# Earlier evacuation of one retention key group, a feed-forward product kept in SBUF, and a reordered exit

## The chip, the cores and the metric

The kernel runs on one core of one Trainium2 chip. The metric is the time of one execution in microseconds, as the median of three runs. The engines are PE (TensorE, with weight loads shown apart as PEld), DVE (VectorE), ACT (ScalarE), POOL (GpSimd) and SP (SyncE, which issues most transfers).

## The reference

A trunk of two layers over 512 tokens of 1024 channels, in float32. Each layer projects the normalised input once, gives the columns to four token mixers of 256 channels each, projects their outputs back and adds them; then a SwiGLU feed-forward part of 2816 hidden channels.

```python
for l in range(DEPTH):                      # DEPTH = 2
    h = rms_norm(x, norm_mix_w[l])
    proj = h @ w_in[l]
    (rq, rk, rv, rg, ca, cg, gq, gk, gv, gg, gb, ga, hq, hf, hi, hgate) = split(proj)
    ret  = head_group_norm(retention_mixer(rq, rk, rv)) * silu(rg)
    conf = conformer_conv_mixer(ca, cg, ...)          # glu, 31 causal taps, layer norm, swish
    gdn  = head_rms_norm(gated_deltanet_mixer(...)) * silu(gg)
    hg   = head_rms_norm(hgrn2_mixer(hq, hf, hi, ...)) * silu(hgate)
    x = x + concat([ret, conf, gdn, hg]) @ w_out[l]
    h = rms_norm(x, norm_ffn_w[l])
    x = x + (silu(h @ ffn_w_gate[l]) * (h @ ffn_w_up[l])) @ ffn_w_down[l]
return rms_norm(x, final_norm_w)
```

## The kernel before

Activations lie with the channels on the 128 partitions and the 512 tokens along the free axis, so a group of 256 channels is two tiles (rk0 and rk1, rq0 and rq1, and so on). Each dense product is made of three matmuls on operands split into a high and a low part: high by high, high by low, low by high (lines 461 to 463; lines 486 to 488 in the form with tokens on the partitions, used for gg, hi, hgate, rv and rg). ScalarE makes the high part of a weight (lines 257 and 383), POOL or VectorE the low part (258 and 384).

**The order of a layer's front.** The projections run in a fixed list, gk, gq, gg, gv, hf, hq, hi, ca0, cg0, ca1, cg1, hgate, rk0, rk1, rq0, rq1, rv, rg. The four mixers gdn (delta rule), hgrn, conf (convolution) and ret (retention) are generators; inside a dense product, after each two contraction steps, `tick()` lets every running mixer write one more step. So the mixers' small products are written in between the dense ones. A mixer starts when its last input is there, ret behind rv. A scheduler that works from its own model of durations then settles the order of instructions on each engine.

**Buffers.** Eight PSUM banks: four of pool `pd` for dense results, four of pool `pm` for all else. conf keeps the glu that its taps read in a `pd` bank too. Tiles in SBUF come from an arena with a size limit; before a dense result is evacuated, the table `NEED` says how many tiles of 2 or 4 KB a partition must be free, by the first two letters of the group's name. If they aren't, `tick()` is called until they are, so mixers' steps come ahead of that evacuation. `rk=(2, 2, 2, 2)` asks for four tiles: cosine and sine by the norm's root, made once at rk0, and two tiles for the rotation. At rk1 the first two exist already.

**The steps that the prediction names.** Rotation of a retention group (`ev_rot`): four ScalarE copies of 32 partitions (727, 728), the product with the cosine on VectorE (729), two POOL operations (730, 731). conf's taps for one half of its channels: 23 operations on VectorE that read the glu (1292), seven on ScalarE (1296) with sums on POOL (1298), and the sum of both (1302). The delta rule's rounds that solve its triangular system: 1051, 1055 and 1062 on TensorE, with copies on VectorE (1057) and ScalarE (1053, 1065) between. Retention's state and outputs: 1387, 1417, 1422, 1429. Norm of a mixer's output: small factors on POOL (213, 771, 775), the product on POOL (781), the gate on VectorE (783), and the turn back to channels on partitions on TensorE (792); then the output projection starts.

**The feed-forward step.** `step` makes a pair of products of two block matrices with seven products in place of eight (Strassen's scheme as changed by Winograd): e, t1, t2, g, h, t3, t4. It runs 52 times, 26 in each layer. `ab` and `cd` are two `pm` banks, LO and UP their halves of 256 columns. t4 of a step is put off: `finish()` writes it behind the first two products of the next step. ScalarE copies t1 from `ab` to `cd` (1650), and the sum of e, t2 and t3 to a tile u3 (1659), which VectorE adds to the upper half of `cd` (1660).

**The exit.** `leave(half)` spreads the root of the norm over the partitions for 256 tokens (two matmuls at 242, a ScalarE copy at 246), multiplies eight tiles (five on VectorE from PSUM, three on POOL from SBUF) and sends each out with a transfer of 128 KB, on ScalarE's and SP's queues by turns.

Of the kernel before, what the change touches and what calls it, by code (L numbers as in the profile page):

```python
# [7 lines left out]
F32 = mybir.dt.float32  # L8
# [8 lines left out]
P = 128  # L17
T = 512
NB = T // P
D = 1024  # L20
KD = D // P
# [117 lines left out]
def kernel(  # L139
# [14 lines left out]
    nc = tc.nc  # L154
    V, S, GP, PE = nc.vector, nc.scalar, nc.gpsimd, nc.tensor
    MUL, ADD, SUB = ALU.mult, ALU.add, ALU.subtract
# [23 lines left out]
    x = [const.tile([P, T], F32, name=f"x{k}") for k in range(KD)]  # L180
# [4 lines left out]
    rsb = const.tile([P, T], F32, name="rsb")  # L185
# [40 lines left out]
    def rstd_sum(blocks, *tiles):  # L226

        ps = pm.tile([P, T], F32, name="pm")
        for n, t in enumerate(tiles):
            for b in blocks:  # L230
                PE.matmul(ps[:, b:b + 1], t[:, b * P:(b + 1) * P], ones[:, 0:1], start=(n == 0 and b == blocks[0]),
                          stop=(n == len(tiles) - 1 and b == blocks[-1]))
        r = slice(blocks[0], blocks[-1] + 1)
        ms = sm(NB, "ms")
        V.tensor_scalar(ms[:, r], ps[:, r], 1.0 / D, 1e-6, op0=MUL, op1=ADD)
        rsqrt_small(rst[:, r], ms[:, r], len(blocks))

    def rstd_spread(blocks=range(NB), half=True):

        pb = pm.tile([P, T], F32, name="pm")  # L240
        for b in blocks:
            PE.matmul(pb[:, b * P:(b + 1) * P], rst[:, b:b + 1].broadcast_to([P, P]), ident, start=True, stop=True)
        if half:
            V.tensor_scalar(rsh, rst, 0.5, None, op0=MUL)
        c = slice(blocks[0] * P, (blocks[-1] + 1) * P)
        S.copy(rsb[:, c], pb[:, c])
        return pb
# [194 lines left out]
    def start(l, name, gen):  # L442
        active.append([gen, (l, name), 0, lag_of((l, name), 0)])
# [5 lines left out]
    def tick():  # L449
        for it in list(active):  # L450
            if it[3] > 0:
                it[3] -= 1
            elif resume(it[0], it[1] + (it[2],)) == "end":
                active.remove(it)
            else:
                it[2] += 1
                it[3] = lag_of(it[1], it[2])
# [7 lines left out]
    def dense_c(ah, al, ks, ps=None):  # L465

        hv = w_next()
        if ps is None:
            ps = pd.tile([P, T], F32, name="pd")
        for n in range(KD):  # L470
            mm3(ps, *hv[n // 4], n % 4, ah[ks[n]], al[ks[n]], n == 0, n == KD - 1)
            if n % CHUNK_K == CHUNK_K - 1:
                tick()
        return ps
# [17 lines left out]
    def dense_c2():  # L492

        hv = [w_next(q) for q in range(2)]
        ps = [pm.tile([P, T], F32, name="pm") for _ in range(2)]
        for k in range(KD):
            for q in range(2):
                mm3(ps[q], *hv[q][k // 4], k % 4, xh[k], xl[k], k == 0, k == KD - 1)
            tick()
        return ps  # L500

    def dense_t(n):

        banks = [pd.tile([P, T], F32, name="pd") for _ in range(NB // 2)]
        ps = {b: (banks[b // 2][:, (b % 2) * n:(b % 2) * n + n], b % 2 == 0, b % 2 == 1) for b in range(NB)}
        for g in range(2):
            t_part(ps, w_next(), n, g, range(NB))
        return {b: ps[b][0] for b in range(NB)}

    def dense_t_wide(n):  # L510

        hv = []
        for part in range(2):
            blocks = range(2 * part, 2 * part + 2)
            ps = {b: (pd.tile([P, T], F32, name="pd")[:, :n], True, True) for b in blocks}
            for g in range(2):
                if part == 0:
                    hv.append(w_next(g))
                elif g:
                    w_ahead()  # L520
                t_part(ps, hv[g], n, g, blocks)
            yield {b: ps[b][0] for b in blocks}
# [9 lines left out]
    for k in range(KD):  # L532
        if k % 4 == 0:
            for p in range(2):
                c = slice(k * P, (k + 4) * P)
# [74 lines left out]
    def layer(l, ar, ga, open_mix, gvp, gzp):  # L610
# [56 lines left out]
        def ev_gg(ps4):  # L667
            if "bt" not in st:
                st["bt"], st["z"], st["gg"] = sm(NB * H, "bt"), sm(NB * H, "z"), ar.get(4)
            bt, z = st["bt"], st["z"]  # L670
            gate_t(ps4, st["gg"])
            for b in ps4:
                S.activation(bt[:, b * H:(b + 1) * H], ps4[b][:, G:G + H], AF.Tanh, scale=rsh[:, b:b + 1])
                V.scalar_tensor_tensor(z[:, b * H:(b + 1) * H], ps4[b][:, G + H:G + 2 * H], rst[:, b:b + 1],
                                       vc[:, o + V_DT:o + V_DT + H], op0=MUL, op1=ADD)
# [731 lines left out]
        def ret_blocks(rk, rq, v, kT, og, pt, scores):  # L1407
            S0 = None
            for b in range(NB):
# [31 lines left out]
                if b % 2 == 1:  # L1441
# [5 lines left out]

        after = {max(("gg", "gv1"), key=ORDER.index): ("gdn", gdn), "hi": ("hgrn", hgrn), "cg1": ("conf", conf), "rv": ("ret", ret)}
        NEED = dict(gg=(4,), hi=(4,), hg=(4,), rv=(4,), rg=(4,), hf=(4, 4, 2, 2), hq=(4,), ca=(2,), cg=(2, 2),
                    rk=(2, 2, 2, 2), rq=(2, 2))  # L1450
        pend = []
        for n, nm in enumerate(ORDER):
            if nm == "gg":
                while not ar.can(*NEED[nm]):
                    tick()
                for ps in dense_t_wide(G + 2 * H):
                    ev_gg(ps)
                continue
            elif nm in T_GROUPS:
                ps = dense_t(G)  # L1460
            elif l == 0 and n < 2:
                if n == 0:
                    first = dense_c2()
                ps = first[n]
            else:

                ps = dense_c(xh, xl, range(KD), pm.tile([P, T], F32, name="pm") if n < 2 else None)
            pend.append((nm, ps))
            if n == R_SUM[l]:
                rstd_sum(range(NB), ssq)  # L1470
            if n < R_SUM[l] + 1:
                continue
            if n == R_SUM[l] + 1:
                rstd_spread()
            for nm, ps in pend:
                while not ar.can(*NEED.get(nm[:2], ())):
                    tick()
                ev[nm](ps)
                if nm in after:
                    q, f = after[nm]  # L1480
                    start(l, q, f())
            pend = []
# [9 lines left out]
    for l in range(DEPTH):  # L1492
# [9 lines left out]
        ar = Arena(pool("arena"), x)  # L1502
# [37 lines left out]
        with tc.tile_pool(name=f"ffp{l}", bufs=1, reuse_waits="tile") as ffp, \  # L1540
# [3 lines left out]
            HC = T // 2  # L1544
            LO, UP = slice(0, HC), slice(HC, T)
# [90 lines left out]
            def step(of, first, second):  # L1636

                def product(ps, nm, start=False):
                    hi, lo = w_next()
                    for k in range(KD // 2):  # L1640
                        mm3(ps, hi, lo, k, *of(k, nm), start and k == 0, k == KD // 2 - 1, True)

                ab = pm.tile([P, T], F32, name="pm")
                cd = pm.tile([P, T], F32, name="pm")
                gs = fft.tile([P, T], F32, name="gs")
                u3 = fft.tile([P, HC], F32, name="u3")
                product(cd[:, LO], "e", True)
                S.copy(gs[:, LO], cd[:, LO])
                product(ab[:, UP], "t1", True)
                S.copy(cd[:, UP], ab[:, UP])  # L1650
                finish()
                product(cd[:, LO], "t2")
                S.copy(gs[:, UP], cd[:, LO])
                product(ab[:, LO], "g")
                product(ab[:, UP], "h")
                V.tensor_tensor(ab, ab, gs, op=ADD)
                first(ab)
                product(cd[:, LO], "t3")
                S.copy(u3, cd[:, LO])
                V.tensor_tensor(cd[:, UP], cd[:, UP], u3, op=ADD)  # L1660

                def end():
                    product(cd[:, LO], "t4")
                    second(cd)
                last.append(end)
# [21 lines left out]

                    last.append(lambda: hidden_split(HEAD + PART * (part + 1)))

            def leave(half):  # L1690

                c = slice(half * T // 2, (half + 1) * T // 2)
                pb = rstd_spread(range(2 * half, 2 * half + 2), False)
                for k in range(KD):
                    if k % 3 == 1:
                        GP.tensor_tensor(x[k][:, c], x[k][:, c], rsb[:, c], op=MUL)
                    else:
                        V.tensor_tensor(x[k][:, c], x[k][:, c], pb[:, c], op=MUL)
                    (nc.sync if k % 2 else nc.scalar).dma_start(out[k * P:(k + 1) * P, c], x[k][:, c])

            def down_plain(rows):
                order = plain_order(l, rows)
# [35 lines left out]
            if l + 1 == DEPTH:  # L1738

                rstd_sum(range(NB // 2, NB), ssq, sq)  # L1740
                leave(0)
                leave(1)


def pack(inputs):
# [81 lines left out]
```

## Time and profile before

| | before |
|---|---|
| median of three runs | 1335.5 us (1333.13 to 1335.95) |
| profiled execution | 1333.43 us |
| its span | 1331.6 us |
| mean granted clock of TensorE | 0.978 |
| share of the span: PE, DVE, ACT, POOL | 97%, 67%, 53%, 59% |

The 1.8 us between the profiled execution's time and its span lie outside the profile's first and last instruction. In the timeline a row has the start and the duration in us, the engine, the line, the output tile and its inputs, and in brackets how long the engine had stood idle and what released it. In the rows by stretch the columns are the length, then the busy time and number of instructions of PE, PEld, DVE, ACT and POOL, the granted clock as a share of full, the transfers' share and GB/s.

### The profile page before, as it was taken

What the parts mean: (1) busy time and instruction counts of PE and PEld (TensorE: products, weight loads), DVE (VectorE), ACT (ScalarE), POOL (GpSimd) and SP (SyncE); (2) the same over time, 40 slices, a digit from 0 to 9 for tenths busy, and PEclk for the clock granted to TensorE, in tenths of its full rate; (3) what the DMA queues carried; (4) which work ended last, traced back from release to release, by engine and by line L of the source; (5) the groups of instructions that cost most, each with busy time, mean ns of one, the idle gap of its engine ahead of it and who ended that gap; (6) DMA issues with size and microseconds to landing.
All of it is one profiled execution on the core that took longest, in us unless ns stands there. A gap on an engine that the chain in (4) does not pass through costs nothing.

```text
span 1331.6 us, 23717 instructions
## 1 busy us (share of the span) xinstructions
PE 1287.8 (97%) x8984; PEld 1177.3 (88%) x8984; DVE 897.5 (67%) x1569; ACT 705.5 (53%) x1454; POOL 788.4 (59%) x669
## 2 busy tenths in 40 slices
PE   8999998899999999999999999999999999999996
PEld 6888887888889999999888889889788999999995
DVE  5753778646787867876465448686559777678645
ACT  5553543535456656655545435445444665566554
POOL 6376773753255765676545767747523666566762
PEclk9999998899999999999999999889999999999998
DMA  7223210134043333342542232002423243333322
GB/s 270 79 79 105 75 25 9 41 111 134 25 135 96 111 112 96 97 126 80 164 138 80 81 88 67 25 1 71 154 69 103 80 123 102 110 97 110 122 78 72
DMA packets 60386, 124.52 MB, mean 94 GB/s; under 512 B 17520, under 2 KB 26992, under 8 KB 60272
## 3 DMA queue, kind: packets, MB, share of 16 engines
q1 hardware_dynamic: 58832, 121.83, 30.0%
q8 instruction: 71, 1.16, 0.4%
q10 hardware_dynamic: 1440, 1.18, 0.3%
q14 instruction: 43, 0.35, 0.1%
HBM read 116.17 MB, written 6.82 MB: 92 GB/s over the span
## 4 chain that ended last, share of the span: by engine, by line
PE 82%; DVE 8%; POOL 5%; ACT 3%; issue 2%; DMA 0%; SPq 0%; POOLq 0%; ACTq 0%; DVEq 0%
PE pm L461 12%; PE pm L462 12%; PE pm L463 12%; PE pd L461 10%; PE pd L462 10%; PE pd L463 10%; PE pd L486 2%; PE pm L1189 2%; PE pd L488 2%; PE pd L487 2%; POOL wlo L258 2%; DVE x L1292 1%; PE pm L928 1%; ACT whi L383 1%; PE pm L1062 1%
## 5 line engine op out<-in xcount | busy, mean ns | idle before, releaser
L258 POOL TENSOR_TENSOR wlo<-wraw,whi 128x512 fp32r<-128x512 f32 (+2 forms) x192 | 248.9, 1305 | 227.3 <-ACT whi L257 186.7
L384 POOL TENSOR_TENSOR wlo<-wraw,whi 128x512 fp32r<-128x512 f32 x208 | 272.5, 1329 | 104.4 <-ACT whi L383 99.9
L461 PE MATMUL pm<-bh,whi 128*128 128x256 f32 x1008 | 282.5, 282 | 3.9 <-ACT pm L1650 2.0
L462 PE MATMUL pm<-bl,whi 128*128 128x256 f32 x1008 | 281.2, 280 | 0.0
L463 PE MATMUL pm<-bh,wlo 128*128 128x256 f32 x1008 | 276.5, 280 | 0.0
L257 ACT CAST whi<-wraw 128x512 fp32r<-128x512 f32 (+2 forms) x212 | 125.3, 598 | 188.1 <-PE pd L462 105.1
L461 PEld LDWEIGHTS pm<-bh,whi 128*128 128x128 f32 x1008 | 189.6, 188 | 6.8 <-DVE pm L1660 3.1
L462 PEld LDWEIGHTS pm<-bl,whi 128*128 128x128 f32 x1008 | 190.0, 188 | 0.5
L463 PEld LDWEIGHTS pm<-bh,wlo 128*128 128x128 f32 x1008 | 187.8, 189 | 0.1
L383 ACT CAST whi<-wraw 128x512 fp32r<-128x512 f32 x208 | 126.7, 624 | 50.1 <-PE pm L462 42.7
L461 PE MATMUL pd<-xh,whi 128*128 128x512 f32 x384 | 151.6, 396 | 0.6 <-DVE x L729 0.6
L463 PE MATMUL pd<-xh,wlo 128*128 128x512 f32 x384 | 151.9, 396 | 0.0
L462 PE MATMUL pd<-xl,whi 128*128 128x512 f32 x384 | 151.6, 396 | 0.0
L384 DVE TENSOR_TENSOR wlo<-pd,whi 128x512 fp32r<-128x512 f32 x156 | 107.3, 688 | 52.4 <-ACT whi L383 49.9
L383 ACT CAST whi<-pd 128x512 fp32r<-128x512 f32 x156 | 92.0, 590 | 64.9 <-PE pm L462 22.6
L378 POOL TENSOR_TENSOR wraw<-wraw 128x512 f32<-128x512 f32 x52 | 68.8, 1324 | 78.2 <-DVE pd L366 65.9
L486 PE MATMUL pd<-whi,xh 128*128 128x256 f32 (+1 forms) x320 | 94.2, 295 | 8.0 <-DVE x L1292 3.4
L487 PE MATMUL pd<-wlo,xh 128*128 128x256 f32 (+1 forms) x320 | 93.7, 293 | 0.0
L488 PE MATMUL pd<-whi,xl 128*128 128x256 f32 (+1 forms) x320 | 93.5, 293 | 0.0
L461 PEld LDWEIGHTS pd<-xh,whi 128*128 128x128 f32 x384 | 72.3, 188 | 16.7 <-DVE x L729 0.8
L462 PEld LDWEIGHTS pd<-xl,whi 128*128 128x128 f32 x384 | 72.2, 188 | 16.0
L463 PEld LDWEIGHTS pd<-xh,wlo 128*128 128x128 f32 x384 | 72.2, 188 | 15.9
(359 smaller groups left out, 3181.0 us busy)
## 6 DMA issues: line engine op xcount, KB each, us to landing
wraw<-in_wf_dram SPq DMA_DIRECT2D x88, 512.0 KB, 3.6
wraw<-in_wc_dram SPq DMA_DIRECT2D x34, 512.0 KB, 3.6
wraw<-in_wd_dram SPq DMA_DIRECT2D x32, 512.0 KB, 4.0
wraw<-in_wt_dram SPq DMA_DIRECT2D x16, 512.0 KB, 3.6
wraw<-in_wo_dram SPq DMA_DIRECT2D x32, 256.0 KB, 2.6
x<-in_xt_dram SPq DMA_DIRECT2D x16, 256.0 KB, 3.7
wraw<-in_wd_dram SPq DMA_DIRECT2D x16, 256.0 KB, 2.7
wraw<-in_wd_dram SPq DMA_DIRECT2D x20, 128.0 KB, 2.0
```

The source lines that it names most:

```text
L257: S.copy(hi[:, :n], r)
L258: eng.tensor_tensor(lo[:, :n], r, hi[:, :n].bitcast(F32), op=SUB)
L378: GP.tensor_tensor(src, c, a, op=SUB)
L383: S.copy(hi, src)
L384: eng.tensor_tensor(lo, src, hi.bitcast(F32), op=SUB)
L461: PE.matmul(ps, hi[:, w], ah, start=first, stop=False, skip_group_check=shared)
L462: PE.matmul(ps, hi[:, w], al, start=False, stop=False, skip_group_check=shared)
L463: PE.matmul(ps, lo[:, w], ah, start=False, stop=last, skip_group_check=shared)
L486: PE.matmul(o, xh[k][:, tk], hi[:, w], start=(k == 0 and first), stop=False)
L487: PE.matmul(o, xh[k][:, tk], lo[:, w], start=False, stop=False)
L488: PE.matmul(o, xl[k][:, tk], hi[:, w], start=False, stop=(k == KD - 1 and last))
L1189: PE.matmul(ps[:, (bb * 2 + ct) * P:(bb * 2 + ct + 1) * P], k[:, ct * T + b * P:ct * T + (b + 1) * P], qx[:, (ct * NB + b) * P:(ct * NB + ...
```

## The change

1. `NEED` gets an entry of its own for rk1, two tiles of 2 KB; the lookup tries the full name first, then the two letters.
2. In `step` t1 goes to a tile in SBUF, p5, and no longer to `cd`; after t3 VectorE adds p5 to the lower half of `cd`, read from PSUM, and writes the upper half. The copy to u3 is gone, in each of 52 steps.
3. `leave` spreads both halves' roots first and then multiplies both; the second half's last tile goes from POOL to VectorE.

```diff
--- before.py
+++ after.py
@@ -1447,7 +1447,7 @@
 
         after = {max(("gg", "gv1"), key=ORDER.index): ("gdn", gdn), "hi": ("hgrn", hgrn), "cg1": ("conf", conf), "rv": ("ret", ret)}
         NEED = dict(gg=(4,), hi=(4,), hg=(4,), rv=(4,), rg=(4,), hf=(4, 4, 2, 2), hq=(4,), ca=(2,), cg=(2, 2),
-                    rk=(2, 2, 2, 2), rq=(2, 2))
+                    rk=(2, 2, 2, 2), rk1=(2, 2), rq=(2, 2))
         pend = []
         for n, nm in enumerate(ORDER):
             if nm == "gg":
@@ -1473,7 +1473,7 @@
             if n == R_SUM[l] + 1:
                 rstd_spread()
             for nm, ps in pend:
-                while not ar.can(*NEED.get(nm[:2], ())):
+                while not ar.can(*NEED.get(nm, NEED.get(nm[:2], ()))):
                     tick()
                 ev[nm](ps)
                 if nm in after:
@@ -1643,11 +1643,11 @@
                 ab = pm.tile([P, T], F32, name="pm")
                 cd = pm.tile([P, T], F32, name="pm")
                 gs = fft.tile([P, T], F32, name="gs")
-                u3 = fft.tile([P, HC], F32, name="u3")
+                p5 = fft.tile([P, HC], F32, name="u3")
                 product(cd[:, LO], "e", True)
                 S.copy(gs[:, LO], cd[:, LO])
                 product(ab[:, UP], "t1", True)
-                S.copy(cd[:, UP], ab[:, UP])
+                S.copy(p5, ab[:, UP])
                 finish()
                 product(cd[:, LO], "t2")
                 S.copy(gs[:, UP], cd[:, LO])
@@ -1656,8 +1656,7 @@
                 V.tensor_tensor(ab, ab, gs, op=ADD)
                 first(ab)
                 product(cd[:, LO], "t3")
-                S.copy(u3, cd[:, LO])
-                V.tensor_tensor(cd[:, UP], cd[:, UP], u3, op=ADD)
+                V.tensor_tensor(cd[:, UP], cd[:, LO], p5, op=ADD)
 
                 def end():
                     product(cd[:, LO], "t4")
@@ -1687,16 +1686,17 @@
 
                     last.append(lambda: hidden_split(HEAD + PART * (part + 1)))
 
-            def leave(half):
-
-                c = slice(half * T // 2, (half + 1) * T // 2)
-                pb = rstd_spread(range(2 * half, 2 * half + 2), False)
-                for k in range(KD):
-                    if k % 3 == 1:
-                        GP.tensor_tensor(x[k][:, c], x[k][:, c], rsb[:, c], op=MUL)
-                    else:
-                        V.tensor_tensor(x[k][:, c], x[k][:, c], pb[:, c], op=MUL)
-                    (nc.sync if k % 2 else nc.scalar).dma_start(out[k * P:(k + 1) * P, c], x[k][:, c])
+            def leave():
+
+                pbs = [rstd_spread(range(2 * half, 2 * half + 2), False) for half in range(2)]
+                for half, pb in enumerate(pbs):
+                    c = slice(half * T // 2, (half + 1) * T // 2)
+                    for k in range(KD):
+                        if k % 3 == 1 and (half == 0 or k < KD - 1):
+                            GP.tensor_tensor(x[k][:, c], x[k][:, c], rsb[:, c], op=MUL)
+                        else:
+                            V.tensor_tensor(x[k][:, c], x[k][:, c], pb[:, c], op=MUL)
+                        (nc.sync if k % 2 else nc.scalar).dma_start(out[k * P:(k + 1) * P, c], x[k][:, c])
 
             def down_plain(rows):
                 order = plain_order(l, rows)
@@ -1738,8 +1738,7 @@
             if l + 1 == DEPTH:
 
                 rstd_sum(range(NB // 2, NB), ssq, sq)
-                leave(0)
-                leave(1)
+                leave()
 
 
 def pack(inputs):
```

How it moves instructions, in layer 0. Names with x_ or ar_ are SBUF tiles. First VectorE around the rotation's product (L729) and conf's second row of taps (L1292 into x_76, closed by L1302). Before, at the end of the taps, where the two L729 are those of rk1 and rq0:

```order
L1292 SCALAR_TENSOR_TENSOR x_76<-pd,hcw,x_76 128x482
L1302 TENSOR_TENSOR x_76<-x_76,x_81 128x511
L729 TENSOR_TENSOR x_81<-pd,x_83 128x512
L729 TENSOR_TENSOR x_78<-pd,x_83 128x512
L1321 BN_STATS cs_2235<-pm 128x6
```

And now, at their beginning, where the first L729 is rk0's and the second rk1's:

```order
L1203 TENSOR_TENSOR ar_3_736<-ar_3_736,ar_10_1391 128x128x4
L729 TENSOR_TENSOR x_82<-pd,x_83 128x512
L729 TENSOR_TENSOR ar_1_2035<-pd,x_83 128x512
L1040 COPY_PREDICATED ar_9_1033<-mk,pm 128x16x16
L1040 COPY_PREDICATED ar_4_644<-mk,pm 128x16x16
L1197 COPY_PREDICATED ar_8_1309<-mk,pm 128x64x8
L1288 TENSOR_SCALAR x_76<-pd,hcw,vc 128x512
L1292 SCALAR_TENSOR_TENSOR x_76<-pd,hcw,x_76 128x504
```

rk1's product has moved from behind the 23 taps and L1302 to a place ahead of the first tap. With it the four ScalarE copies and the two POOL operations move.

TensorE, at the first half of rv (L486 to L488 into `pd`), which needs a `pd` bank. Before, behind the last small products of hgrn and conf:

```order
L1255 MATMUL pm<-ar_6_1196,ar_10_1391 128x128 x2
L1242 MATMUL pm<-ar_6_1196,ar_9_1310 128x64 x4
L1315 MATMUL pm<-cs,x_79 128x128
L1247 MATMUL pm<-hS_177,ar_5_911 128x128 x2
L486 MATMUL pd<-whi,xh_84 128x256
L487 MATMUL pd<-wlo,xh_84 128x256
```

And now, around the delta rule's round at L1055 with 96 by 96 blocks:

```order
L487 MATMUL pd<-wlo,xh_86 128x256
L488 MATMUL pd<-whi,xl_94 128x256
L486 MATMUL pd<-whi,xh_86 128x256
L487 MATMUL pd<-wlo,xh_86 128x256
L1055 MATMUL pm<-cs,ar_9_1033 96x96 x4
L1055 MATMUL pm<-cs,ar_4_644 96x96 x4
L488 MATMUL pd<-whi,xl_94 128x256
L486 MATMUL pd<-whi,xh_87 128x256
```

The first half of rv, 48 matmuls, has moved in between the rounds of small products; it stands in pieces of 17, 20, 4 and 7, of which the piece of 17 ends at the first L1055 and the piece of 20 begins behind the second. In layer 1 the pieces are 19, 22, 6 and 1. The second half of rv stays behind conf's last tap.

TensorE at the start of the output projection, with the delta rule's last turns (L792 of ar_4 and ar_7) and the second block of retention (L1417, L1422, L1429). Before:

```order
L792 MATMUL pm<-cs,ar_4_811 128x128 x2
L792 MATMUL pm<-cs,ar_7_1267 128x128 x4
L792 MATMUL pm<-cs,ar_4_811 128x128 x4
L1417 MATMUL pm<-ar_5_911,x_79 128x64
L1417 MATMUL pm<-ar_5_911,x_76 128x64
L1417 MATMUL pm<-ar_5_911,x_79 128x64
L1417 MATMUL pm<-ar_5_911,x_76 128x64
L1422 MATMUL pm<-rS_179,x_78 128x128
L1422 MATMUL pm<-rS_179,ar_1_2274 128x128
L1429 MATMUL pm<-ar_5_911,ar_10_1391 128x128 x2
```

And now:

```order
L1417 MATMUL pm<-ar_5_911,x_79 128x64
L1417 MATMUL pm<-ar_5_911,x_76 128x64
L1417 MATMUL pm<-ar_5_911,x_79 128x64
L1417 MATMUL pm<-ar_5_911,x_76 128x64
L1422 MATMUL pm<-rS_179,x_81 128x128
L1422 MATMUL pm<-rS_179,x_78 128x128
L1429 MATMUL pm<-ar_5_911,ar_10_1391 128x128 x2
L792 MATMUL pm<-cs,ar_4_811 128x128 x6
L792 MATMUL pm<-cs,ar_7_1267 128x128 x4
```

Retention's products have moved ahead of these turns. Further on, retention's own first turn (four L792 of ar_6) has moved to a place ahead of the projection's matmuls into the next bank, of which 42 stood ahead of it.

In the feed-forward steps the sum of VectorE stands at the place that it had, or a row or two earlier, ahead of a weight's low part (L384) or of an addition to x. On ScalarE's queue at the exit the second copy of L246 stands behind the first transfer, where it stood behind the first four.

## The prediction

> **What bounds the kernel now.** I read the page's busy line first and then the stretches, because an average over the span hides where an engine waits.
>
> ```profile
> PE 1287.8 (97%) x8984; PEld 1177.3 (88%) x8984; DVE 897.5 (67%) x1569; ACT 705.5 (53%) x1454; POOL 788.4 (59%) x669
> PE 82%; DVE 8%; POOL 5%; ACT 3%; issue 2%; DMA 0%; SPq 0%; POOLq 0%; ACTq 0%; DVEq 0%
> ```
>
> ```profile
> core 0: us, PE busy (x) PEld busy (x) DVE busy (x) ACT busy (x) POOL busy (x), PEclk, DMA share, GB/s
> 200.00:300.00 100.00, 89.89 (x651) 82.05 (x650) 64.78 (x124) 42.48 (x82) 56.58 (x56) 0.91 0.17 54
> 500.00:600.00 100.00, 99.13 (x837) 98.43 (x836) 75.28 (x125) 62.40 (x135) 64.68 (x50) 1.00 0.35 106
> 199.00:247.00 48.00, 39.66 (x307) 36.73 (x306) 35.40 (x73) 19.59 (x40) 18.66 (x17) 0.86 0.02 7
> 852.00:892.00 40.00, 35.30 (x265) 32.69 (x264) 32.62 (x65) 16.10 (x33) 13.54 (x11) 0.79 0.03 8
> ```
>
> TensorE sets the time: 97% busy, 82% of the chain. In the feed-forward part (500 to 600) it stands still under 1 us in 100 at full clock; only small waits are left there. The soft spots are the two stretches where the small products of the mixers run: 199 to 247 in layer 0 (48 − 39.66 = 8.3 us idle, clock 0.86) and 852 to 892 in layer 1 (4.7 us idle, clock 0.79). The first edit lies in both. The timeline of layer 0 there:
>
> ```profile
> 202.31 0.75 PE L1062 MATMUL pm<-Vs,ar 32*32 32x32 f32 x16 [1.11 <-DVE ar L1057]
> 235.41 1.48 DVE L1292 SCALAR_TENSOR_TENSOR x<-pd,hcw,x 128x483 f32<-128x483 f32 x2 [0.81 <-ACT x L1296]
> 237.03 0.55 PE L486 MATMUL pd<-whi,xh 128*128 128x256 f32 x1 [3.40 <-DVE x L1292]
> 237.72 0.69 DVE L729 TENSOR_TENSOR x<-pd,x 128x512 f32<-128x512 f32 x1
> 238.24 0.41 PE L488 MATMUL pd<-whi,xl 128*128 128x256 f32 x1
> 238.45 0.41 PE L486 MATMUL pd<-whi,xh 128*128 128x256 f32 x1
> 238.55 1.27 POOL L731 TENSOR_TENSOR x<-x,x 128x512 f32<-128x512 f32 x1 [1.84 <-DVE x L729]
> ```
>
> At 237.03 rv's first matmul has waited 3.40 us for the last of conf's taps (L1292), because all four pd banks are taken: one by conf's glu, the others by rk1, rq0 and rq1. rk1's own evacuation (L729 at 237.72) stands on VectorE behind the taps. After the wait a matmul of rv starts every 0.21 us. In layer 1:
>
> ```profile
> 855.53 1.06 PE L1062 MATMUL pm<-Vs,ar 32*32 32x32 f32 x24 [1.96 <-DVE ar L1057]
> 887.71 1.48 DVE L1292 SCALAR_TENSOR_TENSOR x<-pd,hcw,x 128x483 f32<-128x483 f32 x2
> 889.24 0.38 PE L486 MATMUL pd<-whi,xh 128*128 128x256 f32 x1
> 890.05 0.28 PE L486 MATMUL pd<-whi,xh 128*128 128x256 f32 x1
> 890.17 0.28 PE L487 MATMUL pd<-wlo,xh 128*128 128x256 f32 x1
> ```
>
> There rv starts as the taps end (887.71 + 1.48 = 889.19), with no wait, and at full clock its matmuls are 0.12 us apart.
>
> **First edit, layer 0.** The order shows it acts: rk1's evacuation moves ahead of the taps (VectorE 0.69, four ScalarE copies, two POOL operations), its bank is free early, and the first half of rv, 48 matmuls, goes up between the delta rule's small rounds in pieces of 17, 20, 4 and 7. The second half still waits for the glu bank, so for the last tap. What leaves the path behind 237.03 is 48 × 0.12 = 5.8 us at full clock, 48 × 0.21 = 10.1 at half. Ahead of 237.03 they need that same time and find 8.3 us idle. The price of the place: a round behind a piece starts up to 20 × 0.12 = 2.4 us later, and taps stand on VectorE behind these rounds' copies, so the last tap may come 0 to 2.4 us later; VectorE has 48 − 35.40 = 12.6 us to spare, so I take 1. Of 5.8 to 10.1 I take 8, since about half of those matmuls ran at 0.21: gain 7 at rv's end. What is late next is POOL:
>
> ```profile
> 270.79 1.05 POOL L781 TENSOR_TENSOR ar<-ar,fac_g 128x512 f32<-128x512 f32 x1
> 271.87 0.69 DVE L783 TENSOR_TENSOR ar<-ar,ar 128x512 f32<-128x512 f32 x1 [1.55 <-POOL ar L781]
> 923.68 0.66 PE L792 MATMUL pm<-cs,ar 128*128 128x128 f32 x4 [1.48 <-DVE ar L783]
> ```
>
> POOL works nearly without a break from 238.55 to this L781, for which L783 and the turns L792 wait; in layer 1 TensorE already stands 1.48 us there. Three of its 1.27-us rotations come out of that row, 3.8 us, and the order puts about 2 us of retention's small products ahead of those turns: TensorE, 7 us early, would be held for 7 − 3.8 − 2 = 1.2. Retention's own first turn moves ahead of the projection's matmuls, where I allow 0.3 more. Layer 0: 7 − 1.5 = **5.5 us** less; between 2 (POOL's row passes on little) and 9 (no hold, half clock gone).
>
> **First edit, layer 1.** The same 48 matmuls leave the path: 5.8 us. Ahead they find 4.7 us idle, so 1.1 is paid back at full clock, 10.1 − 4.7 = 5.4 at half: gain 0.4 to 4.7. I take **4 us**: the pieces stand at the waits on L1057, where the longest idle time is. If the filled stretch also runs at full clock it is more: VectorE is busy 32.62 of 40, so at most 7.4. Range 0.4 to 7.4.
>
> ```profile
> 239.00:243.00 4.00, 4.00 (x22) 4.00 (x20) 0.69 (x1) 0.62 (x2) 3.35 (x3) 0.50 0.01 2
> 860.00:864.00 4.00, 4.00 (x26) 3.66 (x26) 2.67 (x4) 1.97 (x4) 2.08 (x2) 0.50 0.00 0
> ```
>
> The granted clock is 0.50 after layer 0's wait, and 0.50 at 860 in layer 1, where TensorE is busy all 4 us and its longest wait before was 1.96. The Trainium skill (TensorE: Matmul & The Clock Gate, Part 1: The HAM clock gate) says that the clock halves after an idle window of about 3.4 us. Layer 0 agrees with that, layer 1 does not. By it taking away the 3.40-us wait would return full clock to the 25 or so matmuls that now run at 0.21, some 25 × 0.09 = 2.3 us that my layer-0 term holds already, and it would give layer 1 nothing.
>
> **Second edit.** These rows carry it:
>
> ```profile
> L461 PE MATMUL pm<-bh,whi 128*128 128x256 f32 x1008 | 282.5, 282 | 3.9 <-ACT pm L1650 2.0
> L461 PEld LDWEIGHTS pm<-bh,whi 128*128 128x128 f32 x1008 | 189.6, 188 | 6.8 <-DVE pm L1660 3.1
> ```
>
> ```profile
> DVE pm L1660 <- ACT u L1659: 22.4, 27, 2.4
> ```
>
> ```profile
> L1650 ACT COPY pm<-pm x52: 357/375/396, 386.2 to 1287.3; 128x256 f32<-128x256 f32 x52
> ...
>   PEld pm L461: 2.8, 4
> ```
>
> ```profile
> L1659 ACT COPY u<-pm x52: 365/372/380, 395.5 to 1296.7; 128x256 f32<-128x256 f32 x52
> ```
>
> ```profile
> L1660 DVE TENSOR_TENSOR pm<-pm,u x52: 418/432/433, 396.0 to 1297.1; 128x256 f32<-128x256 f32 x52
> ...
>   PEld pm L461: 4.2, 10
> ```
>
> In each of 52 steps t4 waits for t3's copy (0.37) and then the sum (0.43); now for the sum alone, on VectorE, without the copy. That is 52 × 0.37 = 19 us less on ScalarE, hidden for the most part, since finish() puts t4 behind two products of the next step. What reaches TensorE is its idle time ahead of L461: 3.9 us by the matmuls, 4.2 + 2.8 = 7.0 by weight loads. t2's wait for L1650 should go whole, since the copy no longer writes t2's bank; L1660's by the 0.37 of each. Between 3.9 and 7.0 I take **5 us**. The sum stands a little earlier in VectorE's row, ahead of some weight differences:
>
> ```profile
> L384 DVE TENSOR_TENSOR wlo<-pd,whi 128x512 fp32r<-128x512 f32 x156 | 107.3, 688 | 52.4 <-ACT whi L383 49.9
> ```
>
> If t3 is late there, differences of 0.69 us queue behind the sum. VectorE idles 24.7 us in 100, which covers it; without that cover it costs, so the term runs from 1 us more to 7 less.
>
> **Third edit.** At the end:
>
> ```profile
> 1324.03 0.37 ACT L246 COPY rsb<-pm 128x256 f32<-128x256 f32 x1 [2.40 <-POOL x L1696]
> 1324.48 2.10 POOL L1696 TENSOR_TENSOR x<-x,rsb 128x256 f32<-128x256 f32 x3 [0.68 <-ACT rsb L246]
> ```
>
> ```profile
> 1323.00:1324.00 1.00, 0.00 (x0) 0.00 (x0) 0.40 (x2) 0.00 (x0) 0.80 (x2) 0.50 1.02 337
> 1326.00:1327.00 1.00, 0.00 (x0) 0.00 (x0) 0.17 (x1) 0.00 (x0) 0.57 (x1) 0.50 0.88 288
> 1327.00:1328.00 1.00, 0.00 (x0) 0.00 (x0) 0.00 (x0) 0.00 (x0) 0.00 (x0) 0.50 0.75 250
> ```
>
> The second spread's copy no longer waits 2.40 us behind POOL, and one POOL multiplication (2.10 / 3 = 0.70) goes to VectorE. The last product is ready some 1.1 us sooner, but the transfers already run at 337 GB/s; their only slack is the dip at 1326 to 1328, (49 + 87) / 337 = 0.4 us. I take **0.3 us** less, between 0.9 less and 0.6 more (the spread's copy and a transfer issue now stand between each other on ScalarE's queue).
>
> **Sum.** 5.5 + 4 + 5 + 0.3 = 14.8 us less. The profiled execution took 1333.4 (span 1331.6 and 1.8 around it), so 1318.6 in its terms; it stands 2.1 below the median of 1335.5, and against that the sum gives 1320.7. I say 1320. What can't be told from no change in this kernel is about 0.2%, 2.7 us.
>
> **Rivals.**
> 1. *POOL and the last tap keep the projections' gain* (15%). For it: POOL's full row to 270.79 and the 1.48 us in layer 1; against it: three operations leave that row. Then 2 + 0.4 + 5 + 0.3 = 7.7 us less: 1328.
> 2. *The clock stays up* (10%). With matmuls of rv between the rounds neither stretch falls to 0.50: 9 in layer 0 and the 7.4 that VectorE allows in layer 1, 9 + 7.4 + 5 + 0.3 = 21.7: 1314. Against it: at 860 the clock is at half under a fully busy TensorE.
> 3. *The sum holds up weight differences* (7%), on the other side. VectorE takes its row in order; if the sum waits for t3 while a difference that the next product needs stands behind it, TensorE waits up to 0.69. It decides from (5.5 + 4 + 0.3) / 52 = 0.19 us a step upward. In every other step it is 26 × 0.69 = 18 us, less 9.8: 1344. Against it: the sum's place moves by a row or two, and it is ready 0.37 sooner.
> 4. *Nothing reaches the end* (8%): the taps end by as much later as rv's first half came forward (2.4 us a piece), and t4's waits become waits for weights. 1335.
>
> **How the numbers follow.** The forecast has 60%; its own range is 1313 to 1326. The range to 1331 takes in the first rival and part of the fourth, and down to 1311 the second; outside are the third, most of the fourth and the far ends of the terms. Faster by over 0.2%: 60 + 15 + 10 = 85%; within: 8%; slower: 7%.
>
> **What would show it.** Right: 48 matmuls of L486 to L488 among the rounds between 200 and 237; rv's second half starting within 2.4 us of 237 and the output projection about 5 us earlier; no wait of L461 on the copy L1650; the waits ahead of L461 on the sum down by half; the second L246 right behind the first. Wrong: the last L1292 past 240; L792 waiting over 3 us for L783; L461 or L463 waiting for L384 where they didn't before. The prediction falls if these new waits add up to more than the 14.8.

## The result, and the profile after

The changed kernel takes 1301.9 us, the median of four runs (1300.8 to 1304.6), against 1335.1 for the kernel before, measured beside it. The ratio is 0.9757, with a 95% interval of 0.9737 to 0.9776: 30 to 35 us less. The prediction said 1320, and its range ended at 1311. The direction was right, the size too small by half.

First the busy line and the chain of the changed kernel's page, then four stretches that answer to those of before (the last two are the same stretches of work, moved ahead with it):

```profile
PE 1269.0 (98%) x8984; PEld 1165.1 (90%) x8984; DVE 894.4 (69%) x1570; ACT 690.0 (53%) x1402; POOL 788.2 (61%) x668
PE 89%; DVE 6%; POOL 2%; ACT 1%; issue 1%; DMA 0%; SPq 0%; DVEq 0%; POOLq 0%; ACTq 0%
```

```profile
200.00:300.00 100.00, 95.07 (x686) 85.50 (x686) 73.25 (x131) 47.62 (x91) 62.30 (x60) 0.98 0.24 75
500.00:600.00 100.00, 100.00 (x850) 100.00 (x849) 76.76 (x125) 60.50 (x127) 69.40 (x53) 1.00 0.38 112
196.00:244.00 48.00, 43.82 (x391) 41.71 (x390) 41.05 (x82) 25.10 (x53) 27.18 (x24) 0.96 0.07 23
829.00:869.00 40.00, 36.66 (x343) 34.12 (x342) 34.05 (x63) 20.87 (x43) 20.91 (x20) 0.96 0.02 8
```

The chain has moved to TensorE (82% to 89%), and POOL's part in it is gone from 5% to 2%. In the mixers' stretches the clock is 0.96 where it was 0.86 and 0.79. In the feed-forward part TensorE now issues 850 matmuls in 100 us, where it issued 837: 1.6% more, though its idle time there was only 0.87 of 100 us before.

The places at which the prediction looked, in the timeline: rv's first matmul in layer 0, the last taps, rv's second half in layer 1 (866.31), and the two waits of the turns L792.

```profile
197.17 0.28 PE L486 MATMUL pd<-whi,xh 128*128 128x256 f32 x1
...
230.21 0.72 DVE L1292 SCALAR_TENSOR_TENSOR x<-pd,hcw,x 128x482 f32<-128x482 f32 x1
231.03 0.69 DVE L1302 TENSOR_TENSOR x<-x,x 128x511 f32<-128x511 f32 x1
...
261.74 0.44 PE L792 MATMUL pm<-cs,ar 128*128 128x128 f32 x2 [0.34 <-DVE ml L794]
...
866.31 0.37 PE L486 MATMUL pd<-whi,xh 128*128 128x256 f32 x1
...
897.76 0.44 PE L792 MATMUL pm<-cs,ar 128*128 128x128 f32 x2 [0.67 <-DVE ar L783]
```

rv begins at 197.17, not at 237.03. The last tap ends at 230.93 in layer 0. TensorE waits for L783, which stands behind POOL's L781, only once, 0.67 us in layer 1; the wait of 0.34 us in layer 0 is for L794, VectorE's low part of a turned result.

Where the 31.8 us between the two spans (1331.6 and 1299.8) went, by the starts of the same dense matmuls (L461 to L463, counted in order) in the two traces:

| stretch | before | after | less | predicted |
|---|---|---|---|---|
| to the 385th (start, first projections) | 175.9 | 172.8 | 3.1 | 0 |
| 385th to 881st (layer 0, rotations to output projection) | 209.8 | 198.2 | 11.6 | 5.5 |
| 881st to 2977th (steps of layer 0) | 251.7 | 247.7 | 3.9 | 5 for both layers' steps |
| 2977th to 3169th (end of its feed-forward part) | 37.9 | 36.4 | 1.5 | 0 |
| 3169th to 3457th (layer 1's first projections) | 103.5 | 103.5 | 0.0 | 0 |
| 3457th to 4101st (layer 1, rotations to output projection) | 266.2 | 260.7 | 5.6 | 4 |
| 4101st to 6121st (steps of layer 1) | 241.7 | 238.1 | 3.6 | with layer 0's |
| 6121st to 6301st (end of its feed-forward part) | 30.9 | 29.4 | 1.5 | 0 |
| 6301st to the end | 14.1 | 13.0 | 1.1 | 0.3 |

The 3.1 us at the start are chance of the two executions. They stand ahead of everything that the edits touch, and over all traces this stretch takes 172.7 to 177.3 us. The rows for L1302 give the start of the first row's last sum as the first number after the durations; here before, after, and the run with the first edit in layer 0 alone:

```profile
L1302 DVE TENSOR_TENSOR x<-x,x x4: 685/692/1105, 166.8 to 889.3; 128x511 f32<-128x511 f32 x4
```

```profile
L1302 DVE TENSOR_TENSOR x<-x,x x4: 682/692/1107, 163.6 to 866.7; 128x511 f32<-128x511 f32 x4
```

```profile
L1302 DVE TENSOR_TENSOR x<-x,x x4: 684/692/1108, 168.1 to 877.0; 128x511 f32<-128x511 f32 x4
```

### The profile page after: what moved, and what is told of

It reads as the page before. It is cut to its first block, busy times and chain, and to the rows that moved or that the text cites. A ratio compares the mean times of both kernels' runs of the same rounds, so it can differ in the third digit from the quotient of the medians.

```text
span 1299.8 us, 23698 instructions
## 1 busy us (share of the span) xinstructions
PE 1269.0 (98%) x8984; PEld 1165.1 (90%) x8984; DVE 894.4 (69%) x1570; ACT 690.0 (53%) x1402; POOL 788.2 (61%) x668
## 4 chain that ended last, share of the span: by engine, by line
PE 89%; DVE 6%; POOL 2%; ACT 1%; issue 1%; DMA 0%; SPq 0%; DVEq 0%; POOLq 0%; ACTq 0%
PE pm L462 14%; PE pm L461 14%; PE pm L463 14%; PE pd L461 10%; PE pd L462 10%; PE pd L463 10%; PE pd L488 3%; PE pd L487 3%; PE pd L486 3%; DVE x L1292 2%; PE pm L1189 1%; PE pm L928 1%; DVE ar L1197 1%; DVE ar L623 1%; POOL wlo L258 1%
## 5 line engine op out<-in xcount | busy, mean ns | idle before, releaser
L384 POOL TENSOR_TENSOR wlo<-wraw,whi 128x512 fp32r<-128x512 f32 x208 | 272.6, 1328 | 105.2 <-ACT whi L383 101.6
L461 PE MATMUL pm<-bh,whi 128*128 128x256 f32 x1008 | 281.1, 281 | 0.0
L463 PE MATMUL pm<-bh,wlo 128*128 128x256 f32 x1008 | 276.4, 280 | 0.0
L461 PEld LDWEIGHTS pm<-bh,whi 128*128 128x128 f32 x1008 | 189.7, 188 | 0.5
L463 PEld LDWEIGHTS pm<-bh,wlo 128*128 128x128 f32 x1008 | 187.7, 189 | 0.1
L461 PE MATMUL pd<-xh,whi 128*128 128x512 f32 x384 | 151.7, 396 | 0.8 <-DVE x L729 0.8
L463 PE MATMUL pd<-xh,wlo 128*128 128x512 f32 x384 | 151.8, 396 | 0.0
L384 DVE TENSOR_TENSOR wlo<-pd,whi 128x512 fp32r<-128x512 f32 x156 | 107.0, 686 | 62.2 <-ACT whi L383 58.0
L486 PE MATMUL pd<-whi,xh 128*128 128x256 f32 (+1 forms) x320 | 92.5, 289 | 4.5 <-DVE z L674 2.6
L488 PE MATMUL pd<-whi,xl 128*128 128x256 f32 (+1 forms) x320 | 93.0, 291 | 0.0
L461 PEld LDWEIGHTS pd<-xh,whi 128*128 128x128 f32 x384 | 72.4, 188 | 16.8 <-DVE x L729 1.0
L463 PEld LDWEIGHTS pd<-xh,wlo 128*128 128x128 f32 x384 | 72.1, 188 | 16.0
```

The costliest lines, as they stand in the source:

```text
L384: eng.tensor_tensor(lo, src, hi.bitcast(F32), op=SUB)
L461: PE.matmul(ps, hi[:, w], ah, start=first, stop=False, skip_group_check=shared)
L463: PE.matmul(ps, lo[:, w], ah, start=False, stop=last, skip_group_check=shared)
L486: PE.matmul(o, xh[k][:, tk], hi[:, w], start=(k == 0 and first), stop=False)
L488: PE.matmul(o, xl[k][:, tk], hi[:, w], start=False, stop=(k == KD - 1 and last))
```

## The experiments

All ratios are to the kernel before, on the same chip; us are the ratio's distance from 1 times 1333, about before's median there (1331.8 to 1333.1).

| run | ratio | 95% interval | us |
|---|---|---|---|
| e1_need: first edit | 0.9847 | 0.9826 to 0.9869 | −20.4 |
| e2_step: second edit | 0.9914 | 0.9894 to 0.9933 | −11.5 |
| e3_exit: third edit | 1.0005 | 0.9990 to 1.0019 | +0.7 |
| e4_need_l0: first edit, layer 0 | 0.9921 | 0.9900 to 0.9943 | −10.5 |
| e9_need_l1: first edit, layer 1 | 0.9922 | 0.9906 to 0.9937 | −10.4 |
| e5_t1_sbuf | 0.9994 | 0.9979 to 1.0010 | −0.8 |
| e6_copy_back | 0.9963 | 0.9942 to 0.9984 | −4.9 |
| e7_rv_held | 0.9963 | 0.9945 to 0.9981 | −4.9 |
| e8_fill | 0.9943 | 0.9921 to 0.9964 | −7.6 |
| e10_taps9 (on the changed kernel) | 0.9835 | 0.9814 to 0.9855 | −22.0 |

### Each edit by itself

The edits are those of the diff, one at a time.

> Only the first edit (two tiles asked for at rk1). Theory A, the terms as the two traces place them: the mixers' stretches gain 11.6 us in layer 0 and 5.5 in layer 1, so about 17 us less than before (ratio 0.987), with hardly any time at half clock between 190 and 240 and between 825 and 870. Theory B, the terms as predicted: 9.5 us less (0.993), and the rest of the 33 us lies in the other edits or in the edits together.

> Only the second edit (t1 kept in SBUF, sum without the copy). Theory A: about 10 us less (0.9925), of which some 4 in each layer's steps and 1.3 at the end of each feed-forward part; the issue rate between 500 and 600 rises from 837 to about 850 matmuls in 100 us. Theory B, as predicted from the idle time before L461: 5 us less (0.996). The stretches at half clock in the mixers stay as before in both.

> Only the third edit (both roots spread first). Theory A, from the trace of the changed kernel, where the last transfer follows the last matmul 1 us sooner: 1 us less (0.999). Theory B, as predicted: 0.3 us less, not to be told from none.

They add up: −20.4 − 11.5 + 0.7 = −31.2, where all three together gave −32.4. The first edit gave 20, not 9.5; the second 11.5, not 5; the third nothing that can be measured. For the first, theory A is the nearer one: its 17 us lie just under the interval of 17.5 to 23.2. For the second it holds (8.9 to 14.1). For the third the interval, 1.3 us less to 2.5 more, agrees with theory B and has A's 1 us at its edge. The 1 us at the end of the changed kernel's trace was chance: four traces without the third edit have 13.0 to 13.2 us there too, five have 13.8 to 14.2, and e3_exit itself has 14.3. In e3_exit's trace the second spread is early, and SP's issues of the transfers take as long as they did:

```profile
1321.95 5.99 SPq L1700 DMA_DIRECT2D out_dram<-x  x8
1322.44 0.37 ACT L246 COPY rsb<-pm 128x256 f32<-128x256 f32 x1 [1.32 <-PE pm L242]
```

From the first copy L246 to the end of the span it is 1331.3 − 1320.75 = 10.6 us there, and 1331.6 − 1321.26 = 10.4 before.

### The first edit by layer

```diff
-rk1=(2, 2)
+rk1=(2, 2) if l == 0 else (2, 2, 2, 2)      # e4_need_l0
+rk1=(2, 2, 2, 2) if l == 0 else (2, 2)      # e9_need_l1
```

> The first edit in layer 0 alone; layer 1 asks for four tiles at rk1 as before. Theory A: 11 to 12 us less (0.991), and half clock still in layer 1's stretch. Theory B: 5.5 us less (0.996).

> The first edit in layer 1 alone; layer 0 asks for four tiles at rk1 as before. If the edit's parts add up: the first edit alone less layer 0 alone, 20 less 10, so 8 to 10 us less than before (0.993), with little half clock in layer 1's stretch and 14 us or more of it in layer 0's. If layer 1's gain in the first trace came from layer 0: under 3 us.

Each layer gives about 10 us, and together 20.9, the whole edit's 20.4. So the layers gain alike, where the prediction set 5.5 and 4, and where the table above had 11.6 and 5.6. Single traces differ by some us in each of these stretches: the first edit alone went through layer 0's in 196.5 us and layer 1's in 257.5, 13.3 and 8.7 less than before. Without the edit in a layer, six traces have a mean of 209.6 us (206.3 to 212.5) in layer 0's stretch and 268.7 (266.2 to 273.7) in layer 1's; with it, three have 197.1 and 259.6. That is 12.5 and 9.1 less, 21.6 together. Of e9_need_l1's expectation on the clock one half failed: layer 0's stretch, with four tiles asked for as before, had 6.8 us at half clock, not 14 or more.

### Moved work, or what it does to the clock

Two kernels with the first edit hold rv back behind the taps again: VectorE writes one column of rv's first bank from the last tap's result. The second puts 48 matmuls a layer that add nothing where rv's first half stood.

```diff
 banks = [pd.tile([P, T], F32, name="pd") for _ in range(NB // 2)]
+if hold:                                   # for rv; e8_fill alone has this loop
+    for k in range(KD):
+        for _ in range(3):
+            PE.matmul(banks[0][:, :256], xh[k][:, :P], xl[k][:, :256], start=True, stop=True)
+            PE.matmul(banks[0][:, 256:], xh[k][:, P:2 * P], xl[k][:, 256:], start=True, stop=True)
+if hold:                                   # both; hold() is the tile of the second row of taps
+    V.tensor_copy(banks[0][:, :1], hold()[:, T - 1:])
```

> The first edit alone, but a VectorE write into rv's first bank that reads the last tap's result holds all of rv behind conf's taps, as before; rk1's evacuation stays early. If the gain comes from rv's matmuls standing between the rounds: nearly all of it goes, 0 to 4 us less than before, and the half clock of before is back. If it comes from the earlier evacuation (work taken from POOL, ScalarE and VectorE after the taps): 8 us less or more.

> As the run with rv held, and in the places between the rounds where rv's first half stood, 48 matmuls a layer that add nothing (products of x's two parts, overwritten by rv). rv still comes whole behind the taps, so no work is moved, 96 matmuls are added. If a part of the first edit's gain is the clock that busy matmuls keep up: the taps end about 2.6 us sooner in each layer than with rv held and the small products run at full clock, 4 to 8 us less than with rv held. If only the moved work counts: the same time as with rv held, or up to 5 us more.

With rv held, 15.5 of the 20.4 us are gone: rv's place between the rounds is most of the gain, and the early evacuation by itself gives 4.9 (2.5 to 7.3), a little more than the 0 to 4 of that reading. The half clock of before comes back only in part: 6.8 and 10.2 us in the second rows of taps of the two layers, where it was 7.7 and 17.1.

Something more than moved work is seen at conf's second row of taps. It begins with L1288 and ends with L1302 (other line numbers in the longer kernels); the last two numbers of a row are the starts of the first and the last of four, so the second row in layer 1 took 889.3 − 848.9 = 40.4 us before, 36.1 in the changed kernel, 41.1 with rv held, and 36.2 with the useless matmuls. The rows, in this order, those of L1302 of before and after standing above:

```profile
L1288 DVE TENSOR_SCALAR x<-pd,hcw,vc x4: 798/810/815, 129.8 to 848.9; 128x512 f32<-128x512 f32 x4
```

```profile
L1288 DVE TENSOR_SCALAR x<-pd,hcw,vc x4: 797/808/811, 126.7 to 830.6; 128x512 f32<-128x512 f32 x4
```

```profile
L1290 DVE TENSOR_SCALAR x<-pd,hcw,vc x4: 799/810/811, 128.2 to 841.5; 128x512 f32<-128x512 f32 x4
```

```profile
L1304 DVE TENSOR_TENSOR x<-x,x x4: 684/693/1111, 163.7 to 882.6; 128x511 f32<-128x511 f32 x4
```

```profile
L1295 DVE TENSOR_SCALAR x<-pd,hcw,vc x4: 800/810/814, 127.9 to 843.9; 128x512 f32<-128x512 f32 x4
```

```profile
L1309 DVE TENSOR_TENSOR x<-x,x x4: 684/692/1100, 164.9 to 880.1; 128x511 f32<-128x511 f32 x4
```

The eleven traces with these taps (before, after, and all experiments but e10_taps9) have 22 such second rows: with no dense matmuls in between they took 39.4 to 43.4 us (14 rows), with matmuls, useful or not, 35.9 to 36.3 (7 rows), and 38.0 once, in the changed kernel's layer 0, with 3.4 us of half clock in it (as in two rows of 36.3 and 35.9). One suspect is the clock. Here are the stretches of layer 1, 37 us ahead of rv's part behind the taps, before, after, with rv held, and with the useless matmuls:

```profile
852.00:889.00 37.00, 32.30 (x242) 29.85 (x240) 31.05 (x63) 13.70 (x29) 12.38 (x10) 0.77 0.03 8
```

```profile
829.00:866.00 37.00, 33.66 (x318) 31.12 (x317) 32.02 (x59) 18.67 (x39) 19.28 (x18) 0.95 0.02 8
```

```profile
846.00:883.00 37.00, 28.82 (x238) 26.53 (x238) 32.22 (x63) 15.59 (x35) 12.63 (x11) 0.86 0.03 8
```

```profile
843.00:880.00 37.00, 32.45 (x320) 29.72 (x320) 32.61 (x61) 19.02 (x40) 18.64 (x17) 1.00 0.03 8
```

With 320 matmuls in place of 238 the clock is 1.00, not 0.86. But the clock alone doesn't explain the shorter row. Two rows of layer 0 have the same 3.4 us at half clock: the one of e9_need_l1, without dense matmuls, took 40.0 us, the one of e4_need_l0, with them, 36.3.

```profile
196.33:236.34 40.01, 31.11 (x289) 27.35 (x287) 34.71 (x66) 16.09 (x36) 15.00 (x14) 0.96 0.03 8
```

```profile
197.56:233.84 36.28, 33.56 (x322) 31.11 (x321) 32.11 (x62) 18.84 (x40) 18.23 (x16) 0.95 0.03 8
```

VectorE has four operations less in the second one, 62 for 66. They are hgrn's L1264. The ends of the two rows, e9_need_l1 first:

```profile
227.85 1.21 DVE L1264 SCALAR_TENSOR_TENSOR hS<-hS,hlast,pm 64x64 f32<-64x64 f32 x4
231.27 1.17 DVE L1264 SCALAR_TENSOR_TENSOR hS<-hS,hlast,pm 64x64 f32<-64x64 f32 x4
236.34 0.69 DVE L1302 TENSOR_TENSOR x<-x,x 128x511 f32<-128x511 f32 x1
```

```profile
231.77 1.21 DVE L1264 SCALAR_TENSOR_TENSOR hS<-hS,hlast,pm 64x64 f32<-64x64 f32 x4
233.84 0.69 DVE L1302 TENSOR_TENSOR x<-x,x 128x511 f32<-128x511 f32 x1
235.17 1.17 DVE L1264 SCALAR_TENSOR_TENSOR hS<-hS,hlast,pm 64x64 f32<-64x64 f32 x4
```

In all 14 rows without dense matmuls the eight L1264 stand ahead of the last sum; in all 8 rows with them, e8_fill's included, four stand behind it. So the scheduler settled another order on VectorE too, which takes 1.2 us out of the row by itself, and the useless matmuls changed order and clock together. VectorE's idle time within the row is 5.3 to 9.6 us without dense matmuls and 3.5 to 5.3 with them. In layer 0 six traces without matmuls have VectorE's row in the very same order, and there more half clock does go with a longer row: 40.0 us at 3.4 us of half clock, 40.6 to 40.9 at 7.5 to 7.9, 43.2 at 13.7 and 43.4 at 17.8. In layer 1 it doesn't: 39.7 to 41.1 at 10.2 to 17.1, in orders that differ from trace to trace. So it is shown that matmuls between the rounds shorten the row, useful or not; how much of that is the clock and how much the order on VectorE stays open.

For the whole time no gain from the useless matmuls is shown: e8_fill ends 2.7 us ahead of e7_rv_held by the ratios, less than the 4 to 8 of one reading and not the equal or longer time of the other, and the two intervals overlap. In e8_fill's layer 0, 1.3 us go again at L792's wait and a stretch at half clock falls into the output projection. So the split of the 20.4 stays an estimate: 96 matmuls moved at 0.117 us are 11.2, and two rows of taps that end 4 us sooner are 8, which makes 19. That leaves next to nothing for the 4.9 of the early evacuation, so the terms overlap or are too large.

### The two parts of the second edit

```diff
-S.copy(cd[:, UP], ab[:, UP])
+S.copy(p5, ab[:, UP])                                        # e5_t1_sbuf
...
 S.copy(u3, cd[:, LO])
-V.tensor_tensor(cd[:, UP], cd[:, UP], u3, op=ADD)
+V.tensor_tensor(cd[:, UP], u3, p5, op=ADD)                   # e5_t1_sbuf
```

```diff
 S.copy(p5, ab[:, UP])
+S.copy(cd[:, UP], ab[:, UP])                                 # e6_copy_back, on e2_step
```

> From before: t1 is copied to SBUF and no longer into t2's bank, but t3 is still copied by ScalarE before VectorE adds the two. It takes away only the wait of t2 on the copy L1650. If that wait is what the second edit removes: 4 to 6 us less than before. If the chain behind t3 (copy, then sum) is: 2 us less or under.

> The second edit alone, with one more ScalarE copy of t1 into the upper half of t2's bank (its values are overwritten by the sum). The sum still comes without a copy behind t3, but t2's bank is written by ScalarE again as before. If the bank is what the second edit frees: half or more of its gain is gone. If the chain behind t3 is: the gain of the second edit alone but for 1 or 2 us.

By the starts of the dense matmuls, where chance hardly enters (the feed-forward part runs at full clock in all traces), the second edit takes 7.5 us from the two layers' steps and 2.9 from the two ends of the part, 10.5 in all. With only t1 in SBUF it is 0.6 and 2.7; with the sum without a copy, but t2's bank written, 6.3 and 1.2. So in the steps the chain behind t3 is nearly everything, by e6_copy_back, and at the ends t2's bank, which the copy no longer writes. e6_copy_back's second reading came out for the steps. e5_t1_sbuf is the weaker test, since it does more than its expectation says: with both inputs in SBUF the sum took 1.29 us in the median, where it took 0.43 before (and 0.43 in e6_copy_back).

```profile
L1661 DVE TENSOR_TENSOR pm<-u,u x52: 423/1286/1624, 393.8 to 1296.5; 128x256 f32<-128x256 f32 x52
```

So its 0.6 us is what freeing t2's bank gave less what the slower sum cost, and the bank's share in the steps is bounded by the other run: 7.5 − 6.3 = 1.2 us. The whole times, −0.8 and −4.9, are each about 2.5 us worse than these sums (−3.4 and −7.5); both traces have more half clock elsewhere than before's (55 and 58 us ahead of the exit, where it is 48), which no part of these edits explains. What the steps gain shows in the rate of issue; here the rows from 1060 to 1160 of before, e5_t1_sbuf, e6_copy_back and after:

```profile
1060.00:1160.00 100.00, 99.08 (x835) 98.35 (x834) 72.54 (x123) 61.17 (x132) 66.60 (x51) 1.00 0.37 112
```

```profile
1060.00:1160.00 100.00, 99.73 (x839) 98.91 (x839) 80.41 (x123) 61.67 (x133) 67.79 (x51) 1.00 0.36 111
```

```profile
1060.00:1160.00 100.00, 100.00 (x850) 100.00 (x849) 74.36 (x125) 62.92 (x134) 66.06 (x51) 1.00 0.36 112
```

```profile
1060.00:1160.00 100.00, 100.00 (x851) 100.00 (x851) 73.78 (x122) 59.15 (x124) 66.86 (x51) 1.00 0.35 108
```

835, 839, 850 and 851 matmuls. The waits of e5_t1_sbuf say what is left there: the sum, slower and still behind the copy. At the ends no wait of a matmul on L1568 is left, and 0.5 us by the weight loads.

```profile
PEld pm L461 <- DVE pm L1661: 6.0, 16, 0.8
```

And before, the wait at the ends, which the prediction didn't count to this edit:

```profile
PE pd L461 <- ACT ph L1568: 2.3, 2, 1.2
```

There t4 of the last step stood in TensorE's row behind nearly all plain products that can do without it (the last of its matmuls ends at 654.1 us), and the first that needs its channels came at once:

```profile
655.48 1.19 PE L461 MATMUL pd<-ph,whi 128*128 128x512 f32 x4 [1.17 <-ACT ph L1568]
```

In the changed kernel's order t4 stands sooner, with 16 matmuls of the plain products between it and that place in each layer, and the wait is gone.

### Fewer taps on VectorE

```diff
-CONF_POOL = 7
+CONF_POOL = 9
```

> The changed kernel with nine of conf's 30 later taps on ScalarE and POOL and 21 on VectorE, where it has seven and 23. If VectorE's last tap still sets when rv's second half starts: two taps of 0.72 us less in each layer's second row, 1 to 3 us less than the changed kernel's 1302, so 1299 to 1301. If POOL's chain, or TensorE's own rounds, set the end there: the same as the changed kernel, or 1 to 4 us more.

Worse: 1310 us, and by the ratios (0.9835 and 0.9757) some 10 us over the changed kernel, more than either reading allowed. The second row of taps got longer in layer 1, 39.3 us where it was 36.1, with no half clock in it at all; in layer 0 it took 37.9, as long as before this change (38.0), in spite of two taps less. The first row in layer 0 took 40.6, where the others have 35.5 to 37.0. So the number of VectorE's operations doesn't set the last tap by itself. Two things changed beside it: all eight L1264 stand ahead of the last sum again, and the turns wait longer for POOL's row, through L783, 1.99 us in layer 0 and 2.15 in layer 1:

```profile
261.80 0.63 PE L792 MATMUL pm<-cs,ar 128*128 128x128 f32 x4 [1.99 <-DVE ar L783]
```

Where the 10 us lie is not shown: the mixers' stretches took 198.1 and 261.6 us (198.2 and 260.7 in the changed kernel), and of the 7.7 us between the two spans 4.5 stand ahead of the 385th dense matmul, where traces differ by as much through chance. The changed kernel stays the fastest measured.

## Why the prediction was wrong

**Which bank and which wait** was right: 48 matmuls of rv stand between the rounds in each layer, the second half begins behind the last tap, the waits of L461 on L1650 and L1660 are gone, and the second L246 comes 1.25 us behind the first (2.77 before). None of the signs that the prediction gave for being wrong came: it failed in sizes, in terms that it had set too low.

**Layer 0, 5.5 predicted, 10.5 measured (e4_need_l0).** Two steps failed. "The last tap may come 0 to 2.4 us later ... I take 1": it came sooner, since the row of taps shrank by 2.8 us in the changed kernel and by 4.5 in e1_need. The price that the prediction put on the pieces, rounds and with them taps that come later, is not to be seen: VectorE's idle time in the row fell from 6.6 to 5.3 and 4.2 us, and four L1264 left the row. Clock and order both have a part in that, as said above. And "TensorE would be held for 7 − 3.8 − 2 = 1.2" behind POOL, with 0.3 more at retention's turn: the waits of L792 are 0.34 us there, and not for POOL. Of the first rival nothing was left.

**Layer 1, 4 predicted, 10.4 measured (e9_need_l1).** The step that failed is "1.1 is paid back at full clock, 5.4 at half". Nothing to speak of was paid back. The 48 matmuls went in between and the row of taps still got shorter, from 40.4 to 36.1 us; the filled stretch ran at 0.95 of the clock in the changed kernel and at full clock in e1_need. The prediction had higher clock as its second rival, at 10%, with 7.4 us as the most that VectorE allows. The 10.4 of the ratios (8.4 to 12.5) and the 9.1 of the traces lie above that bound. The bound took VectorE's work ahead of the last tap as fixed, and four operations of that work went behind the tap. That rival's total, 1314, was still 12 us above what was measured, most of it through the second edit.

**Second edit, 5 predicted, 11.5 measured, 10.5 by the trace.** "Between 3.9 and 7.0 I take 5": the steps gave 7.5, so the waits of the weight loads were the term, and the idle time of the matmuls was too low a bound. A matmul is busy 0.28 us and the next one follows 0.117 later, so a delay of up to 0.16 us leaves no idle time in that row. The issue rate, 837 in 100 us at a pitch of 0.117 (98 us of work), would have shown 2 us in 100; so would the weight loads' share in the same row, 98.43 of 100. The other 3 us are at the ends, a row (2.3 us in two waits) that stood in the answer on waits and wasn't traced back to t4.

**Third edit, 0.3 predicted.** A gain of that size can't be told from none. The second copy came sooner, and the end stayed where it was.

**The rivals.** The third (the sum holds up weight differences) and the fourth didn't occur: in the changed kernel no wait of L461 or L463 on L384 is among the page's groups.

## What to carry over

Where matmuls overlap, read a stretch's rate of issue against the pitch; the busy share hides delays shorter than a matmul's duration. Independent dense work put between small dependent products can gain more than its own time, when what waits for these products on other engines comes sooner too; here a row of taps ended some 4 us sooner. Before a higher clock is called the reason, compare rows of equal clock, and look whether the scheduler has also changed the order on the other engines. And one buffer asked for too early can hold a bank whose next user is what would have filled the gap.

## What the runs showed of the hardware

In layer 1's stretch without dense matmuls the clock was at half for 17.1 us in three traces (before, e2_step, e3_exit) and for 10 to 14 in four (e4 to e7). With 48 matmuls of 256 columns in between, it was at half for 0 to 3.4 us, also where the matmuls were useless. The pieces at half clock ahead of the exit are 3.4 us long or a multiple of it in every trace, which agrees with the window that the Trainium skill names (TensorE: Matmul & The Clock Gate, Part 1: The HAM clock gate); that an idle window must come first does not agree with layer 1. Here are the 3.4 us ahead of two pieces at half clock in before:

```profile
853.97:857.38 3.41, 1.85 (x31) 1.81 (x32) 3.25 (x8) 0.51 (x2) 1.80 (x2) 1.00 0.16 42
147.41:150.82 3.41, 3.41 (x57) 3.35 (x56) 3.26 (x7) 1.44 (x5) 3.41 (x4) 1.00 0.84 248
```

In layer 1 TensorE was busy 1.85 of 3.41 us, with no wait of over 1.96. In the other place it was busy throughout; 48 of the 57 matmuls there were products of 32 by 32 blocks or of two columns. What makes the clock fall in such places was not tried.

With both inputs in SBUF VectorE's sum of 128x256 took 1.29 us in the median (e5_t1_sbuf), and 0.43 with one input in PSUM (before, e6_copy_back). Why was not tried either.
